# Which engine splits the weights and adds the compression offsets in a two-layer fp32 trunk: GpSimd's shares of the first mixer and of the MLP starts given to VectorE

## The chip, the cores and the metric

One NeuronCore of a Trainium2 chip runs the whole program. Its engines each work through an own queue in order: TensorE (PE; PEld is its weight load), VectorE (DVE), ScalarE (ACT), GpSimd (POOL), and SyncE (SP), which here issues the weight DMAs. Semaphores tie the queues together. The metric is the device time of one execution in microseconds, lower is better.

## The reference

The trunk has 256 tokens of width 1024 and two layers. Each layer is a token mixer and a squared-ReLU MLP, each behind an RMS norm whose scale, shift and gate come from a conditioning vector. The first mixer is a sparse attention with a compressed branch; the second is a differential attention, which the change does not touch. The parts that matter here:

```python
def compress_blocks(blk, pe, w1, w2):          # blocks of 32 tokens, one every 16
    z = (blk + pe[:, None, :]).transpose(0, 1, 3, 2, 4).reshape(B, NC, NSA_GROUPS, CMP_BLOCK * HEAD_DIM)
    return jax.nn.silu(z @ w1) @ w2
...
for i in range(DEPTH):
    mod = cond @ w_ada[i] + b_ada[i]
    ...
    x = x + g1[:, None, :] * y                  # y: the mixer's output
    h = rms_norm(x, ln_mlp_g[i]) * (1.0 + sc2[:, None, :]) + sh2[:, None, :]
    x = x + g2[:, None, :] * (jnp.square(jax.nn.relu(h @ w_mlp_in[i])) @ w_mlp_out[i])
```

Everything is fp32. `compress_blocks` is called once for keys and once for values; there are 15 blocks, 4 groups.

## The kernel before

**Split weights.** An fp32 product is made of three matmuls over halves. `mm3` (L78 to L83) issues them: L81 is high half times high half, L82 and L83 are the two cross products; the name on the right of an `out<-in` says which tiles they read. A weight tile `wr` (128x1024 fp32, 512 KB) comes by a DMA that SP issues. `do_unit` (L190 to L233) turns it into a "unit": the high half `wh` is a cast on ACT (L202), the low half `wl` is `wr` minus `wh`, one `tensor_tensor` (L206), on VectorE or on GpSimd. Which of the two is read from the list `halves[0]`: split number p takes entry p modulo the length of the list. `use(u)` (L241) hands a unit to the matmuls and first splits the units that lie up to `look[0]` ahead, so a split is emitted some units before its product. Splits carry a lowered priority; the Tile scheduler then fixes one order per engine, and that order is what the queues run.

**Where the list stands before.** `sublayer_end` sets `[(act.copy, vec)]` at the end of each sublayer: VectorE alone. Before each mixer the main program sets two entries, so every second split goes to POOL. `mlp` sets three entries with one on POOL ahead of `up_first(nb)`, which computes the first two 512-wide blocks of the hidden layer.

**The first mixer.** `proj_rows` multiplies the normed input by the weight units; `kv_post` (L900) norms and rotates keys (`head_norms` L796, L805 to L814; `rope` L775, L781 to L785; statistics `hns`, `hnm`, `hnt`, `hnr`), computes the gates (`gz`, `gates`, L894 to L898) and transposes the keys on PE (`heads_T`, L793). `compress` (L912) makes `z`, the block inputs plus offsets (L917 memset, L920 sums), multiplies them (L927) and applies the activation (`he`, L931 to L933). Attention scores follow, with `mn` (L1014), `pr` (L1043) on DVE. The vector `acc` of the conditioning projection is summed in between from its own weight tiles on DVE (L227, L232): `acc` plus `wr` times a column, tile after tile, in DVE's order.

**The MLP start.** `prenorm` (L1143) norms the residual per token half t and in quarters: L561 to L572 (statistics `lnss`, POOL's power `lnr` at L570, scaled rows at L572), PE transposes (L1151), scale and shift (L1156 on DVE, L1159 on ACT), then `hh` (high half, L1163) and `hl` (low half, L1164). `up_first` multiplies them block by block, L81 to L83 with out `sc`, transposes the activated blocks back (L1229) and splits them (L76 on ACT, L77 on DVE, out `z`).

All tiles of 128x1024 (`wh`, `wl`, `z`, `acc`) come from one ring of 32.

Of the kernel before, what the change touches and what calls it, by code (L numbers as in the profile page):

```python
# [23 lines left out]
ALU = mybir.AluOpType  # L24
# [3 lines left out]
P = 128  # L28
# [14 lines left out]
def body(ctx: ExitStack, tc: tile.TileContext, a):  # L43
    nc = tc.nc
    vec, act, pool, pe = nc.vector, nc.scalar, nc.gpsimd, nc.tensor
# [9 lines left out]
    def bank(tag="tr"):  # L55
        return pp.tile([P, 512], F32, name=tag, tag=tag, bufs={"acc": 4, "sc": 2, "tr": 2}[tag])

    def tmp():
        return tp.tile([P, 512], F32, name="t", tag="t", bufs=6)

    def w4(name, dt=F32):

        return wp.tile([P, 1024], dt, name=name, tag="w", bufs=32)
# [4 lines left out]
    def z4():  # L68
        return w4("z4", F32R).rearrange("p (i s) -> p i s", i=4)

    def small(shape, name, bufs=3, dt=F32):
        return sp.tile(shape, dt, name=name, tag=name, bufs=bufs)
# [18 lines left out]
    halves = [[(act.copy, vec)]]  # L91
# [149 lines left out]
    def use(u, only=False):  # L241

        ahead = look[0] if only else 0
        for v in range(u, len(units)):
            if units[v][0] == "w":
                ahead += 1
                if v > u and ahead > look[0] - 1:
                    break
            done_to(v)
            if only:  # L250
                break
        h, l = done.pop(u)
        return lambda c, w: (h[:, c : c + w], l[:, c : c + w])
# [48 lines left out]
    def rsqrt_mean(ss, w, shape, name, bufs=3):  # L302

        m, r, t = (small(shape, name + c, bufs) for c in "mrt")
        vec.tensor_scalar(m, ss, 1.0 / w, EPS, op0=ALU.mult, op1=ALU.add)
        act.activation(t, m, AF.Ln)
        act.activation(r, t, AF.Exp, scale=-0.5)
        vec.tensor_tensor(t, r, r, op=ALU.mult)
        vec.tensor_tensor(t, t, m, op=ALU.mult)
        vec.tensor_scalar(t, t, -0.5, 1.5, op0=ALU.mult, op1=ALU.add)  # L310
        vec.tensor_tensor(r, r, t, op=ALU.mult)
        return r
# [344 lines left out]
    def kv_products(k):  # L657
        wu = [done.pop(u) for u in U["kv", k]]

        def w_(c, n):  # L660
            return tuple(z[:, c % 1024 : c % 1024 + n] for z in wu[c // 1024])

        st, sp_ = k == 0, k == KT - 1
        x_ = hh[:, k], hl[:, k]
        for bk, c0 in ((b_kc, 0), (b_vc, 256)):
            for m in range(2):
                mm3(bk[:, m * S : (m + 1) * S], w_(c0 + m * P, P), x_, st and m == 0, sp_)
        yield
        for t in range(2):
            ts = slice(t * P, (t + 1) * P)  # L670
            x_ = hh[:, k, ts], hl[:, k, ts]
            mm3(b_ks[:, t * 256 : t * 256 + 256], x_, w_(512, 256), st and t == 0, sp_)
            mm3(b_m[t][:, 0:256], x_, w_(768, 256), st, sp_)
            mm3(b_m[t][:, 256:512], x_, w_(1024, 256), False, sp_)
            mm3(b_v[t][:, 0:304], x_, w_(1280, 304), st, sp_)
            yield

    kc2 = []
# [59 lines left out]
    for k in range(KT):  # L738
        g = kv_products(k)
# [29 lines left out]
    pe2 = (cols[:, 0:16], cols[:, 16:32])  # L769
# [142 lines left out]
    def compress():  # L912

        hb = bank()
        for kv in range(2):
            z = w4("z").rearrange("p (m g c) -> p m g c", m=16, g=4)
            pool.memset(z[:, :, :, 15], 0.0)  # L917
            for mh in range(2):
                for g in range(4):
                    pool.tensor_tensor(z[:, 8 * mh : 8 * mh + 8, g, 0:15],  # L920
                                      kc2[kv][:, g, 8 * mh : 8 * mh + 120].rearrange("p (c m) -> p m c", m=8),
                                      pe2[kv][:, 8 * mh : 8 * mh + 8][:, :, None].to_broadcast([P, 8, 15]), op=ALU.add)
            zs.append(z)
            yield 0
        for m in range(16):
            for kv in range(2):
                pe.matmul(hb[64 * kv : 64 * kv + 64, 0:P], zs[kv][:, m].rearrange("p g c -> p (g c)"),  # L927
                          w1c[2 * kv + m // 8][:, m % 8], start=m == 0, stop=m == 15, skip_group_check=True)
        he = small([P, P], "he", 1)
        act.activation(he, hb[:, 0:P], AF.Exp, scale=-1.0)  # L930
        vec.tensor_scalar(he, he, 1.0, None, op0=ALU.add)  # L931
        vec.reciprocal(he, he)
        vec.tensor_tensor(he, hb[:, 0:P], he, op=ALU.mult)  # L933
        yield 1
        tb = bank()
        pe.transpose(tb[:, 0:P], he, ident)
        hid = small([P, 4, 16], "hid", 1)
        vec.tensor_copy(hid.rearrange("p g c -> p (g c)"), tb[:, 0:64])
        hidv = tmp()[:, 0:256].rearrange("p (q i c) -> p q i c", q=2, i=4)
        vec.tensor_copy(hidv, tb[:, 64:P].rearrange("p (q c) -> p q c", q=2)[:, :, None, :].to_broadcast([P, 2, 4, 32]))  # L940
        yield 1
        kb = bank()
        for h in range(2):
            pe.matmul(kb[64 * h : 64 * h + 64, 0:32], w2c[0], hid.rearrange("p (gp h) c -> p h gp c", h=2)[:, h],
                      start=True, stop=True, skip_group_check=True)
        sq = small([P, 32], "csq", 1)
        act.activation(sq, kb[:, 0:32], AF.Square)

        for gp in range(2):
            vb = bank()  # L950
            pe.matmul(vb[:, 0:64], hidv[:, gp].rearrange("p i c -> p (i c)"), w2c[1], start=True, stop=True)
            vec.tensor_tensor(vt[gp][:, 512:1024].rearrange("p (e d) -> p e d", e=8),
                              vb[:, 0:64][:, None, :].to_broadcast([P, 8, 64]),
                              own[:, :, None].to_broadcast([P, 8, 64]), op=ALU.mult)
        yield 1
        sb = bank()
        pe.matmul(sb[:, 0:32], bdones, sq, start=True, stop=True)
        rr = rsqrt_mean(sb[:, 0:32], 64, [P, 32], "cr", 1)
        for h in range(2):
            ps_ = slice(64 * h, 64 * h + 64)  # L960
            vec.scalar_tensor_tensor(kcbd[ps_, :, h, :], kb[ps_, 0:32].rearrange("p (g c) -> p g c", g=2),
                                     gk0[ps_], rr[ps_].rearrange("p (g c) -> p g c", g=2), op0=ALU.mult, op1=ALU.mult)
        yield 0
# [232 lines left out]
    def mlp(l):  # L1196
# [4 lines left out]
        def relu2(bk):  # L1201
            r = tmp()
            act.activation(r, bk, AF.Relu)  # L1203
            s2 = tmp()
            act.activation(s2, r, AF.Square)
            return s2

        def up_first(nb):

            zs = [(z4(), z4()) for _ in range(nb)]  # L1210
            hid.update(enumerate(zs))
            ws = {}

            def products(b, t):
                ts = slice(t * P, (t + 1) * P)
                if t == 0:
                    ws[b] = [[use(u) for u in U["up", l, b, f2]] for f2 in range(2)]
                bk = bank("sc")
                for f2 in range(2):
                    for k in range(KT):  # L1220
                        mm3(bk[:, f2 * 256 : f2 * 256 + 256], (hh[:, k, ts], hl[:, k, ts]),
                            ws[b][f2][k // 4](k % 4 * 256, 256), k == 0 and f2 == 0, k == KT - 1)
                return relu2(bk)

            def back(b, t, s2):
                ts = slice(t * P, (t + 1) * P)
                tb = bank()
                for j in range(4):
                    pe.transpose(tb[:, j * P : (j + 1) * P], s2[:, j * P : (j + 1) * P], ident)  # L1229
                split(zs[b][0][:, :, ts], zs[b][1][:, :, ts], tb.rearrange("p (j s) -> p j s", j=4))  # L1230

            prev = None
            for t in range(2):
                for b in range(nb):
                    s2 = products(b, t)
                    if prev is not None:
                        back(*prev)
                    prev = (b, t, s2)
            back(*prev)
# [51 lines left out]
                    yield t, 2  # L1291

        look[0], ahead_dma[0] = 6, 14
        halves[0] = [(act.copy, pool), (act.copy, vec), (act.copy, vec)]
        nb = 2
        up_first(nb)
        while held:
            held.pop(0)()
        for b in range(1, NB):
# [4 lines left out]


    look[0], ahead_dma[0] = 4, 10
    halves[0] = [(act.copy, pool), (act.copy, vec)]
    cg = compress()
    next(cg)
    next(cg)  # L1310
# [194 lines left out]
```

## Time and profile before

| | us |
|---|---|
| median of 3 runs | 722.15 |
| lowest, highest | 720.5, 722.8 |
| the profiled execution, by its own time | 721.25 |
| its span (first to last recorded instruction) | 719.1 |
| PE busy | 682.3 (95%) |
| DVE busy | 493.1 (69%) |
| ACT busy | 400.5 (56%) |
| POOL busy | 200.5 (28%) |

The profiled execution takes 2.15 us more than its span; both parts lie inside its 721.25. Busy shares are means over the whole program; the views by stretch tell where an engine is short. The clock row of the page gives TensorE's granted clock: 1.00 is the upper of its two levels, 2.4 GHz, and 0.50 the lower, 1.2 GHz.

### The profile page before, as it was taken

What the parts mean: (1) busy time and instruction counts of PE and PEld (TensorE: products, weight loads), DVE (VectorE), ACT (ScalarE), POOL (GpSimd) and SP (SyncE); (2) the same over time, 40 slices, a digit from 0 to 9 for tenths busy, and PEclk for the clock granted to TensorE, in tenths of its full rate; (3) what the DMA queues carried; (4) which work ended last, traced back from release to release, by engine and by line L of the source; (5) the groups of instructions that cost most, each with busy time, mean ns of one, the idle gap of its engine ahead of it and who ended that gap; (6) DMA issues with size and microseconds to landing.
All of it is one profiled execution on the core that took longest, in us unless ns stands there. A gap on an engine that the chain in (4) does not pass through costs nothing.

```text
span 719.1 us, 11663 instructions
## 1 busy us (share of the span) xinstructions
PE 682.3 (95%) x4263; PEld 565.1 (79%) x4263; DVE 493.1 (69%) x911; ACT 400.5 (56%) x779; POOL 200.5 (28%) x138
## 2 busy tenths in 40 slices
PE   8999889999988999999999999899979999999997
PEld 7787654656687988999896777667769888998896
DVE  4457879777869598858885987776782874235753
ACT  6646438769565345634453765786566355543650
POOL 4105311002023243233231634223222143323430
PEclk9999999999999999999999999999999999999999
DMA  9999999522828889989799254243744787755001
GB/s 289 331 334 373 325 307 289 150 75 91 263 87 274 279 298 370 331 286 319 262 358 350 81 159 170 94 118 92 243 164 138 261 280 229 231 180 176 1 1 58
DMA packets 105421, 156.67 MB, mean 218 GB/s; under 512 B 6135, under 2 KB 60180, under 8 KB 105364
## 3 DMA queue, kind: packets, MB, share of 16 engines
q1 hardware_dynamic: 103952, 153.60, 65.9%
q0 software_dynamic: 1248, 2.20, 1.1%
q8 instruction: 33, 0.54, 0.3%
q14 instruction: 24, 0.20, 0.1%
q10 hardware_dynamic: 164, 0.14, 0.1%
HBM read 154.86 MB, written 1.06 MB: 217 GB/s over the span
## 4 chain that ended last, share of the span: by engine, by line
PE 59%; DVE 17%; issue 11%; DMA 4%; ACT 4%; POOL 2%; SPq 1%; DVEq 0%; POOLq 0%; ACTq 0%
PE acc L83 9%; PE acc L81 8%; PE acc L82 8%; PE sc L83 8%; PE sc L81 7%; PE sc L82 7%; DVE wl L206 5%; DMA wr<-in_nsa_w_in_dram 3%; DVE acc L232 2%; PE sc L1008 1%; PE tr L172 1%; ACT wh L202 1%; PE tr L1048 1%; SPq L158 1%; POOL wl L206 1%
## 5 line engine op out<-in xcount | busy, mean ns | idle before, releaser
L206 POOL TENSOR_TENSOR wl<-wr,wh 128x1024 fp32r<-128x1024 f32 x60 | 157.5, 2628 | 363.2 <-ACT wh L202 298.0
L206 DVE TENSOR_TENSOR wl<-wr,wh 128x1024 fp32r<-128x1024 f32 (+1 forms) x132 | 188.5, 1443 | 63.3 <-ACT wh L202 46.2
L202 ACT CAST wh<-wr 128x1024 fp32r<-128x1024 f32 x192 | 191.9, 1032 | 47.4 <-PE acc L82 10.0
L81 PE MATMUL acc<-wh,z 128*128 128x512 f32 (+1 forms) x320 | 127.5, 398 | 0.0
L83 PE MATMUL acc<-wh,z 128*128 128x512 f32 (+1 forms) x320 | 125.2, 392 | 1.1 <-DVE z L77 1.1
L82 PE MATMUL acc<-wl,z 128*128 128x512 f32 (+1 forms) x320 | 125.2, 391 | 0.0
L81 PE MATMUL sc<-hh,wh 128*128 128x256 f32 x384 | 109.0, 284 | 0.0
L83 PE MATMUL sc<-hh,wl 128*128 128x256 f32 x384 | 108.7, 283 | 0.0
L82 PE MATMUL sc<-hl,wh 128*128 128x256 f32 x384 | 108.7, 283 | 0.0
L1203 ACT ACTIVATE t<-sc 128x512 f32<-128x512 f32 x32 | 19.1, 598 | 109.6 <-PE sc L83 109.5
L81 PEld LDWEIGHTS sc<-hh,wh 128*128 128x128 f32 x384 | 73.6, 192 | 1.3 <-issue 0.8
L82 PEld LDWEIGHTS sc<-hl,wh 128*128 128x128 f32 x384 | 73.7, 192 | 0.4
L232 DVE SCALAR_TENSOR_TENSOR acc<-wr,cond,acc 128x1024 f32<-128x1024 f32 x49 | 72.4, 1477 | 2.2 <-DMA wr<-in_w_ada_dram 1.5
L83 PEld LDWEIGHTS sc<-hh,wl 128*128 128x128 f32 x384 | 73.6, 192 | 0.0
L83 PEld LDWEIGHTS acc<-wh,z 128*128 128x128 f32 x320 | 60.1, 188 | 14.2 <-DVE z L77 2.0
L81 PEld LDWEIGHTS acc<-wh,z 128*128 128x128 f32 x320 | 60.2, 188 | 13.7 <-issue 1.9
L82 PEld LDWEIGHTS acc<-wl,z 128*128 128x128 f32 x320 | 60.2, 188 | 11.5 <-issue 0.6
L77 DVE TENSOR_TENSOR z<-t,z 128x512 fp32r<-128x512 f32 x24 | 26.7, 1113 | 60.3 <-ACT z L76 60.3
L82 PE MATMUL acc<-wl,hh 128*128 128x512 f32 (+1 forms) x160 | 61.1, 382 | 3.0 <-DVE wl L206 3.0
L81 PE MATMUL acc<-wh,hh 128*128 128x512 f32 (+1 forms) x160 | 63.1, 396 | 0.0
L83 PE MATMUL acc<-wh,hl 128*128 128x512 f32 (+1 forms) x160 | 60.5, 378 | 0.0
L83 PE MATMUL sc<-wh,hl 128*128 128x256 f32 (+1 forms) x152 | 44.1, 292 | 4.2 <-DVE hl L1164 4.1
(286 smaller groups left out, 1119.4 us busy)
## 6 DMA issues: line engine op xcount, KB each, us to landing
wr<-in_w_ada_dram SPq DMA_DIRECT2D x80, 512.0 KB, 5.9
wr<-in_w_mlp_in_dram SPq DMA_DIRECT2D x64, 512.0 KB, 4.9
wr<-in_w_mlp_out_dram SPq DMA_DIRECT2D x64, 512.0 KB, 4.4
wr<-in_diff_w_in_dram SPq DMA_DIRECT2D x24, 512.0 KB, 5.1
wr<-in_w_ada_dram SPq DMA_DIRECT2D x32, 256.0 KB, 6.8
wr<-in_nsa_w_in_dram SPq DMA_DIRECT2D x16, 512.0 KB, 7.3
wr<-in_nsa_w_out_dram SPq DMA_DIRECT2D x16, 256.0 KB, 10.4
wr<-in_diff_w_out_dram SPq DMA_DIRECT2D x8, 512.0 KB, 3.7
```

The lines of the kernel that those rows point to most:

```text
L77: vec.tensor_tensor(l, src, h.bitcast(F32), op=ALU.subtract)
L81: pe.matmul(out, x[0], w[0], start=start, stop=False, skip_group_check=True)
L82: pe.matmul(out, x[0], w[1], start=False, stop=False, skip_group_check=True)
L83: pe.matmul(out, x[1], w[0], start=False, stop=stop, skip_group_check=True)
L158: nc.sync.dma_start(f(raws[i]), src)
L172: pe.matmul(ps[32 * c : 32 * c + 32, 0:n], condz[:, k], w, start=k < 4, stop=k >= 4, skip_group_check=True, tile_position=(0, 32 * c))
L202: hi(h, r[:, 0:n])
L206: lo.tensor_tensor(l, r[:, 0:n], h.bitcast(F32), op=ALU.subtract)
L232: vec.scalar_tensor_tensor(st["acc"], r, c, st["acc"], op0=ALU.mult, op1=ALU.add)
L1008: pe.matmul(p1, q[:, P:S], k, start=True, stop=True)
L1048: pe.transpose(tb[:, e * P : (e + 1) * P], s.pr[:, br, h, e * P : (e + 1) * P], ident)
L1203: act.activation(r, bk, AF.Relu)
```

## The change

Three edits. The sums of the compression are four VectorE instructions of 480 columns instead of sixteen GpSimd instructions of 120 (the memsets of `z` stay on POOL). The list with one POOL entry in three is set behind `up_first` instead of ahead of it, so all splits that `up_first` emits, the units ahead that it looks at too, are VectorE's. The two-entry list ahead of the first mixer is gone; there the list of one entry holds. The second mixer keeps its own.

```diff
             for mh in range(2):
-                for g in range(4):
-                    pool.tensor_tensor(z[:, 8 * mh : 8 * mh + 8, g, 0:15],
-                                      kc2[kv][:, g, 8 * mh : 8 * mh + 120].rearrange("p (c m) -> p m c", m=8),
-                                      pe2[kv][:, 8 * mh : 8 * mh + 8][:, :, None].to_broadcast([P, 8, 15]), op=ALU.add)
+                vec.tensor_tensor(z[:, 8 * mh : 8 * mh + 8, :, 0:15],
+                                  kc2[kv][:, :, 8 * mh : 8 * mh + 120].rearrange("p g (c m) -> p m g c", m=8),
+                                  pe2[kv][:, 8 * mh : 8 * mh + 8][:, :, None, None].to_broadcast([P, 8, 4, 15]), op=ALU.add)
...
         look[0], ahead_dma[0] = 6, 14
-        halves[0] = [(act.copy, pool), (act.copy, vec), (act.copy, vec)]
         nb = 2
         up_first(nb)
+        halves[0] = [(act.copy, pool), (act.copy, vec), (act.copy, vec)]
...
     look[0], ahead_dma[0] = 4, 10
-    halves[0] = [(act.copy, pool), (act.copy, vec)]
     cg = compress()
```

On POOL ten of the 60 splits leave: six in the first mixer and two at each MLP start. Numbers behind names tell apart tiles of one name; the numbering differs between the kernels.

**DVE, keys of the first mixer.** `wl_998` before and `wl_986` after are the low half of the third weight unit of this stretch, `wl_1018` (POOL before) and `wl_1006` that of the fourth. Before:

```order
L897 RECIPROCAL gates_942<-gz_1039 128x48
L898 TENSOR_SCALAR gcmp_943<-gates_942,consts_76 128x16 x2
L308 TENSOR_TENSOR hnt_989<-hnr_988 128x16
L206 TENSOR_TENSOR wl_998<-wr_575,wh_997 128x1024
L309 TENSOR_TENSOR hnt_989<-hnt_989,hnm_987 128x16
L310 TENSOR_SCALAR hnt_989<-hnt_989 128x16
L311 TENSOR_TENSOR hnr_988<-hnr_988,hnt_989 128x16
```

After:

```order
L206 TENSOR_TENSOR wl_917<-wr_569,wh_916 128x1024
L728 TENSOR_TENSOR csg_296<-trig_213,gbg_276 128x64
L919 TENSOR_TENSOR z_951<-t_897,cols_685 128x32x15 x2
L919 TENSOR_TENSOR z_955<-t_902,cols_685 128x32x15 x2
L805 TENSOR_REDUCE hns_961<-t_966 128x4
L805 TENSOR_REDUCE hns_961<-t_969 128x4
L805 TENSOR_REDUCE hns_961<-t_972 128x4
L894 TENSOR_TENSOR gz_1021<-sc_292,gbg_276 128x48
L305 TENSOR_SCALAR hnm_975<-hns_961 128x16
L894 TENSOR_TENSOR gz_1027<-tr_293,gbg_276 128x48
L206 TENSOR_TENSOR wl_986<-wr_575,wh_985 128x1024
L308 TENSOR_TENSOR hnt_977<-hnr_976 128x16
```

The four sums stand ahead of the third unit's split, and the gate work (`gates`, `gcmp`) has moved behind it.

**PE, the same place.** `acc` with `wl_1018` (before) and `wl_1006` (after) are products of the fourth unit, `tr<-first,qn` the transposes of the keys. Before:

```order
L81 MATMUL acc_972<-wh_1017,hh_138 128x512
L793 MATMUL tr_1069<-first_75,qn_974 128x128 x4
L793 MATMUL tr_1078<-first_75,qn_974 128x128 x4
L82 MATMUL acc_972<-wl_1018,hh_138 128x512
L83 MATMUL acc_972<-wh_1017,hl_139 128x512
```

After:

```order
L81 MATMUL acc_959<-wh_1005,hh_138 128x512
L81 MATMUL acc_960<-wh_1005,hh_138 128x512
L81 MATMUL acc_1165<-wh_1041,hh_138 128x512
L82 MATMUL acc_959<-wl_1006,hh_138 128x512
L83 MATMUL acc_959<-wh_1005,hl_139 128x512
L793 MATMUL tr_1057<-first_75,qn_962 128x128 x4
L793 MATMUL tr_1066<-first_75,qn_962 128x128 x4
```

The transposes have moved ahead by five matmuls of 512 columns, to near the start of the fourth unit.

**DVE, start of the first MLP.** The second `hh` and `hl` of the first token half, `t_2350` before and `t_2338` after; `wl_2412` after is the third unit, which was POOL's. Before:

```order
L206 TENSOR_TENSOR wl_2412<-wr_2015,wh_2411 128x1024
L572 TENSOR_SCALAR t_2365<-xt_82,lnr_2363 128x512
L206 TENSOR_TENSOR wl_2418<-wr_2107,wh_2417 128x1024
L1163 CAST hh_138<-t_2350 128x4x128
L1156 TENSOR_SCALAR t_2374<-tr_2369,mA01_131,mB01_132 128x128
L1164 TENSOR_TENSOR hl_139<-t_2350,hh_138 128x4x128
```

After:

```order
L206 TENSOR_TENSOR wl_2400<-wr_2003,wh_2399 128x1024
L563 SCALAR_TENSOR_TENSOR lnss_2296<-lnss_2296 128x1
L206 TENSOR_TENSOR wl_2406<-wr_2095,wh_2405 128x1024
L1162 CAST hh_138<-t_2338 128x4x128
L572 TENSOR_SCALAR t_2353<-xt_82,lnr_2351 128x512
L1163 TENSOR_TENSOR hl_139<-t_2338,hh_138 128x4x128
L206 TENSOR_TENSOR wl_2412<-wr_2148,wh_2411 128x1024
```

The split that was POOL's stands on DVE behind `hl`, not ahead of it. At the second MLP it does too, and PE's order there is as it was.

## Rows read from the trace of the kernel before

**Rows 1.** Windows: stretch, its length, busy of each engine, PEclk, DMA share, GB/s
```profile
70.00:90.00 20.00, 16.35 (x115) 12.87 (x113) 17.20 (x29) 8.94 (x16) 8.95 (x10) 0.91 1.08 323
110.00:130.00 20.00, 18.52 (x104) 10.51 (x104) 17.92 (x92) 17.55 (x67) 2.41 (x1) 1.00 1.06 292
235.00:390.00 155.00, 154.45 (x982) 136.72 (x981) 115.83 (x97) 72.13 (x93) 48.49 (x22) 1.00 0.91 318
```
**Rows 2.** Waits of PE, 55 to 105: us in total, times, longest
```profile
PE acc L82 <- DVE wl L206: 2.4, 2, 1.8
```
**Rows 3.** Waits of PE, 105 to 200
```profile
PE sc L1008 <- DVE mn L1014: 1.1, 2, 0.6
```
**Rows 4.** Waits of PE, 200 to 300
```profile
PE sc L83 <- DVE hl L1164: 1.8, 1, 1.8
PE tr L1229 <- DVE z L77: 1.6, 1, 1.6
PE acc L83 <- DVE z L77: 0.8, 1, 0.8
```
**Rows 5.** Waits of PE, 490 to 560
```profile
PE sc L83 <- DVE hl L1164: 2.3, 2, 1.8
```
**Rows 6.** POOL in order of time: start, us, instruction, idle before and releaser
```profile
64.38 5.41 POOL L920 TENSOR_TENSOR z<-t,cols 128x120 f32<-128x120 f32 x8
74.17 2.37 POOL L206 TENSOR_TENSOR wl<-wr,wh 128x1024 fp32r<-128x1024 f32 x1
...
202.11 2.38 POOL L206 TENSOR_TENSOR wl<-wr,wh 128x1024 fp32r<-128x1024 f32 x1 [1.83 <-ACT wh L202]
```
**Rows 7.** DVE in order of time, first mixer
```profile
67.68 0.48 DVE L728 TENSOR_TENSOR csg<-trig,gbg 128x64 f32<-128x64 f32 x1
...
71.93 1.53 DVE L206 TENSOR_TENSOR wl<-wr,wh 128x1024 fp32r<-128x1024 f32 x1
...
74.28 2.31 DVE L311 TENSOR_TENSOR hnr<-hnr,hnt 128x16 f32<-128x16 f32 x1
...
77.95 1.69 DVE L781 TENSOR_TENSOR ropeA<-qn,csg 128x128 f32<-128x128 f32 x2
79.56 0.48 DVE L781 TENSOR_TENSOR ropeB<-qn,csg 128x128 f32<-128x128 f32 x2
79.97 1.21 DVE L206 TENSOR_TENSOR wl<-wr,wh 128x1024 fp32r<-128x1024 f32 x1
...
95.72 0.17 DVE L311 TENSOR_TENSOR hnr<-hnr,hnt 128x16 f32<-128x16 f32 x1
...
97.24 1.97 DVE L310 TENSOR_SCALAR crt<-crt 128x32 f32<-128x32 f32 x1
...
176.39 3.16 DVE L1043 TENSOR_SCALAR pr<-pr,sm 128x128 f32<-128x128 f32 x4
...
179.80 0.99 DVE L1043 TENSOR_SCALAR pr<-pr,sm 128x128 f32<-128x128 f32 x4
```
**Rows 8.** PE in order of time, at the key transposes
```profile
79.35 0.39 PE L83 MATMUL acc<-wh,hl 128*128 128x512 f32 x1
79.58 0.39 PE L81 MATMUL acc<-wh,hh 128*128 128x512 f32 x1
81.64 1.09 PE L793 MATMUL tr<-first,qn 128*128 128x128 f32 x8 [1.67 <-DVE qn L785]
```
**Rows 9.** DVE in order of time, start of the first MLP
```profile
197.65 0.69 DVE L1164 TENSOR_TENSOR hl<-t,hh 128x512 fp32r<-128x512 f32 x1
...
202.51 2.53 DVE L1164 TENSOR_TENSOR hl<-t,hh 128x512 fp32r<-128x512 f32 x1
...
216.86 2.52 DVE L227 TENSOR_SCALAR acc<-wr,cond 128x1024 f32<-128x1024 f32 x1 [6.61 <-PE sc L83]
```
**Rows 10.** Windows (columns as in Rows 1), the spells below full clock
```profile
76.00:78.00 2.00, 2.00 (x6) 1.52 (x6) 1.97 (x6) 1.04 (x1) 1.66 (x2) 0.50 1.04 377
...
536.00:538.00 2.00, 2.00 (x12) 2.00 (x11) 1.87 (x4) 1.43 (x2) 0.00 (x0) 0.50 0.00 0
```

## The prediction

> **What bounds the kernel now.** I read the windows by stretch first. From 235 to 390, in the body of the first MLP, PE is busy for 154.45 of 155 us at granted clock 1.00 [rows 1]. There POOL and DVE can be as late as they like; what the change moves there is worth nothing. The stretches where PE is short are the mixers and the MLP starts: 16.35 of 20 us between 70 and 90, with DVE at 17.20 and POOL at 8.95, and 18.52 of 20 between 110 and 130, with DVE at 17.92 [rows 1]. Next the waits of PE in those stretches: it waits 2.4 us for low halves of weights between 55 and 105 [rows 2], and 1.67 us for the rotated keys `qn` ahead of their transposes at 81.64 [rows 8]; 1.8 us for `hl`, 1.6 and 0.8 us for `z` at the first MLP's start [rows 4]; 2.3 us for `hl`, one wait 1.8 of it, around the second MLP's start [rows 5]. Every one of these releasers is DVE. Each wait removed with nothing late behind it is time gained.
>
> Then DVE's rows at those waits, to see why DVE is late. The 16-column `hnr` (L311) takes 2.31 us at 74.28, and 0.17 us at 95.72 [rows 7]. POOL splits a weight from 74.17 for 2.37 us, to 76.54 [rows 6]: `hnr` ends at 76.59, just behind it. `hl` takes 0.69 us at 197.65 and 2.53 us at 202.51, ending at 205.04 [rows 9]; POOL splits from 202.11 to 204.49 [rows 6]. So a DVE instruction that starts while POOL works in SBUF stands still until POOL is done. Other rows look the same: `pr` 3.16 us against 0.99 [rows 7], `ropeA` 1.69 against 0.48 for `ropeB` of the same size [rows 7], `crt` at 1.97 [rows 7], L227 at 2.52 [rows 9]. In the trace a POOL split of about 2.4 us costs DVE up to its own length, while the same split as DVE's own work is 1.21 us [rows 7]. This is the argument for a gain: in a stretch where DVE is the releaser, taking a split over can be cheaper for DVE than standing beside POOL's.
>
> Last the windows on the clock. PE runs at 0.50 (1.2 GHz) from 76 to 78 and from 536 to 538 [rows 10]; 2 us at half rate lose 1.0 us of full-rate work. Each follows a wait of PE of 1.8 us, for a low half [rows 2] and for `hl` [rows 5]; the wait of 1.8 us for `hl` at the first MLP [rows 4] and that of 1.67 us for the keys [rows 8] have none behind them. Two of four: I count a spell as even after such a wait.
>
> **The change, part by part. First, the keys of the first mixer (64 to 82).** The sums cost DVE 4 instructions of 480 columns. The nearest row is `hl`, two SBUF inputs and 512 columns, 0.69 us [rows 9]: 480/512 of it is 0.65, so 2.6 us in all. The upper bound comes from POOL: 8 sums take 5.41 us [rows 6], so four, the work of one new instruction, take 2.7; a POOL split takes 2.37 against DVE's 1.21, a ratio of 2, so 1.35 each and 5.4 in all. I take 2.6, because the same-engine row is nearer.
>
> One rule of the Trainium skill speaks against that. The sums read their input with a step of 8 fp32 values, 32 bytes, whereas `hl` reads in a row. The page "SBUF — State Buffer", section "Door 1: The DMA port swizzle", notes 16-byte lines, and that each access that crosses to a new line pays a penalty; here every element would. No row of this trace shows a DVE read with that step; if the penalty doubled the read, an estimate from that page's note would be 1.3 us each, the mixer's term below would become a loss, and the sum would be some 3 us smaller.
>
> Now the chain. Between the end of `csg` (68.16) and the start of the fourth split in DVE's order (79.97) there are 11.8 us, of which the third split is 1.53 [rows 7], so 10.3 us of other work. Of these go the hold on `hnr`, 2.31 − 0.17 = 2.1, and that on `ropeA`, 1.69 − 0.48 = 1.2 [rows 7]. The statistics and gate instructions between 68 and 74 run beside POOL's sums and are slower too; I estimate 1.5 us back on them, with 0 as the bound. That leaves 5.5 us. By the new order the sums go ahead of the third split; from 68.16 it is 2.6 (sums) + 1.2 (third split) + 5.5 = 77.5 for the start of the fourth, 78.7 for its end. Two short instructions follow, so the key transposes start at 79.3 instead of 81.64 [rows 8]. PE's order has put five 512-column matmuls behind them that were in front; two of them in a row start 0.23 us apart [rows 8], so 1.15 us are still to do. Gain 81.64 − 79.3 − 1.15 = 1.2 us. With sums at 5.4 and no 1.5 back, it is 1.2 − 2.8 − 1.5 = −3.1; with the `hnr`-like relief reaching all of it, about +1.7. The wait on the third unit shrinks only a little, and a new wait of some 2 us arises at the fourth unit's low half; it is inside this number. The split that was POOL's at 76.89 now follows the transposes on DVE; PE then has the fourth unit's remaining products to work on, so I count it at nothing, and at 1.2 us if that cover is gone.
>
> **Second, the rest of the mixer (82 to 190).** Four POOL splits become DVE's, 4 × 1.21 = 4.8 us. The one at 97 held `crt` (1.97 us, such small ones take 0.17, so 1.8 back) and the one at 177 held `pr` (3.16 − 0.99 = 2.2 back) [rows 7]: these two gain DVE 1.6 together. The one near 110 falls into DVE at 17.92 of 20 busy [rows 1], where PE waits 1.1 us for `mn` [rows 3]: up to 1.2 lost. The one near 166 I count at nothing, and at 1.2 if PE turns out to wait for it: among the waits of that stretch, of which the longest on DVE are such as `mn`, none is for a split. I take 0 in all, between +1.6 gained and 2.4 lost.
>
> **Third, the first MLP's start.** The hold on `hl` goes: POOL's split of 202.11 is DVE's behind `hl`. The second `hl` would end about 202.6, and the two splits ahead of it in DVE's order stood ahead of it before too. The 1.8 us wait goes [rows 4]. The half-done products of the second token half gain nothing from it: their `hh` comes behind two splits now, but PE has whole blocks of the first half to do. Further on, L227 stood 2.52 us beside POOL's second split [rows 9], and the two `z` waits of 1.6 and 0.8 [rows 4] come behind that on DVE. The split takes 1.21 on DVE instead; about half of 2.4 should go, 1.2, with bounds 0 and 2.4. Together 3.0.
>
> **Fourth, the second MLP's start.** PE's order is the same, and DVE's split has moved behind `hl`: the 1.8 us go [rows 5]. The spell at 0.50 behind it (1.0 us [rows 10]) goes with an even chance, 0.5. Together 2.3. What hides the splits added here is PE's queue of first-half products.
>
> **The sum.** 1.2 + 0 + 3.0 + 2.3 = 6.5 us, off the profiled execution's own 721.25 (span 719.1 and 2.15 around it): 714.7. The median before, 722.15, is 0.9 higher, within the spread of its three runs; I don't shift for that. Nothing after the starts takes it back: the body of the MLP is PE's alone [rows 1].
>
> **Rivals.** *The clock and new waits.* PE meets two waits in the keys' stretch, of about 1 and 2 us, and a spell at 0.50 follows: 1.0 lost. The spell at the second MLP stays, 0.5 less, and the `z` waits stay, 1.2 less. 6.5 − 2.7 = 3.8, so 717.4. For it: two such spells are in the trace [rows 10]. Against: the waits before them are what the change shortens.
>
> *Everything goes.* Mixer 1.7 + 1.6, first MLP 1.8 + 2.4, second 1.8 + 1.0: 10.3, so 710.9. For it: every one of these waits has DVE as its releaser. Against: the mixer's DVE is at 86 to 90% [rows 1], and adds work.
>
> *The sums are dear.* At 1.35 us each the third and fourth splits come late, the keys' stretch loses 3.1, and the rest of the mixer 0.5 more; the MLP starts give only the two `hl` waits, 3.6. Time 721.2: no change.
>
> *DVE becomes the mixer's bound (the slower side).* Six splits, 7.3 us, and sums of 5.4 add 12.7 us to DVE between 64 and 190. If the holds that end give back only `hnr` and `pr` (2.1 + 2.2), as other waits stand ready behind `ropeA` and `crt`, the mixer pays 8.4; less 3.6 from the MLPs, 726.0. It decides from a net mixer cost of 3.6 + 2.2 = 5.8 us on. For it: DVE is 90% busy from 110 to 130 [rows 1]. Against: from 150 on DVE has room, so the splits there hide, and POOL's holds are seen on the very rows.
>
> **How the numbers follow.** Forecast (712 to 716) 0.45; the clock and new waits 0.22; everything goes 0.13; sums dear 0.12; DVE bound 0.08. A measurement of this kernel can tell 0.3%, 2.2 us, from no change. So faster 0.80, same 0.12, slower 0.08. The time is that of the forecast, 714.7. The range from 710.5 to 719.8 leaves out the DVE bound (0.08), most of the dear sums and the low end of everything.
>
> **What would show it.** Right: `hl` near 0.7 us at both MLP starts and no PE wait there; `hnr` near 0.2; the sums at 0.6 to 0.7 us each; key transposes near 79. Wrong: sums above 1 us; a new PE wait of over 2 us on `wl` near 76 with a spell at 0.50 behind it; PE waiting longer for `mn` around 110 to 130, or for `z` at the first MLP.

## The result

| | before | after |
|---|---|---|
| median of 13 runs, us | 722.42 | 716.33 |
| lowest to highest, us | 719.19 to 724.56 | 713.05 to 719.47 |
| the profiled execution, us (span) | 721.25 (719.1) | 713.05 (711.3) |

The ratio is 0.9925, with a 95% interval of 0.9903 to 0.9947: 5.4 us faster, between 3.8 and 7.0. The forecast was 714.7, that is 6.5 us off the profiled execution. The profiled execution of after happens to be its fastest run, so the two traces differ by 8.2 us, more than the kernels do. Places are read from the traces below, the worth of an edit from the timed runs.

The page of after, part 1. To be read against it: DVE had 493.1 us for 911 instructions before.

```profile
PE 678.2 (95%) x4263; PEld 562.3 (79%) x4263; DVE 492.3 (69%) x925; ACT 399.6 (56%) x779; POOL 166.9 (23%) x112
```

DVE took over ten splits (12 us by their own length) and the sums (4 us), and its busy time did not rise. So before, about that much of DVE's busy time was standing still beside POOL.

DVE of after, in order of time, at the places of [rows 7] and [rows 9] (start, us, instruction, idle before and releaser):

```profile
67.96 4.01 DVE L919 TENSOR_TENSOR z<-t,cols 128x480 f32<-128x480 f32 x4
...
75.19 0.12 DVE L311 TENSOR_TENSOR hnr<-hnr,hnt 128x16 f32<-128x16 f32 x1
...
200.73 0.69 DVE L1163 TENSOR_TENSOR hl<-t,hh 128x512 fp32r<-128x512 f32 x1
...
214.50 0.75 DVE L227 TENSOR_SCALAR acc<-wr,cond 128x1024 f32<-128x1024 f32 x1
...
526.98 0.69 DVE L1163 TENSOR_TENSOR hl<-t,hh 128x512 fp32r<-128x512 f32 x1
```

`hnr` takes 0.12 us where it took 2.31, `hl` 0.69 at both MLP starts where it took 2.53, L227 0.75 where it took 2.52. A sum takes 1.00 us. PE's waits of after, 200 to 300, the answer to [rows 4]:

```profile
PE acc L83 <- DVE z L77: 1.0, 1, 1.0
```

The wait for `hl` at the first MLP is gone, and of the 2.4 us for `z` 1.4. For 490 to 560, the answer to [rows 5], one row is of interest: the long wait there is gone, the short one is left.

```profile
PE sc L83 <- DVE hl L1163: 0.5, 1, 0.5
```

And PE's waits from 55 to 105 and 105 to 200, the answers to [rows 2] and [rows 3]:

```profile
PE acc L82 <- DVE wl L206: 4.2, 3, 2.3
...
PE sc L81 <- DVE hh L1162: 2.3, 1, 2.3
PE sc L1007 <- DVE mn L1013: 1.5, 2, 1.0
```

In the first mixer PE waits longer for low halves (4.2 us against 2.4), and at the mixer's end it waits 2.3 us for `hh`. Of before's lists, three rows belong beside these:

```profile
PE tr L793 <- DVE qn L785: 1.7, 1, 1.7
PE tr L793 <- DVE kcbd L961: 1.3, 1, 1.3
...
PE sc L81 <- DVE hh L1163: 1.4, 1, 1.4
```

The waits for the keys `qn` and for `kcbd` (a tile of compressed keys) are gone, so up to 105 the three kinds together, 5.4 us, became 4.2. The wait for `hh` was 1.4. PE of after at the key transposes, the answer to [rows 8]:

```profile
74.24 0.50 PE L82 MATMUL acc<-wl,hh 128*128 128x512 f32 x1 [2.32 <-DVE wl L206]
...
78.90 0.50 PE L82 MATMUL acc<-wl,hh 128*128 128x512 f32 x1 [1.42 <-DVE wl L206]
...
79.47 1.04 PE L793 MATMUL tr<-first,qn 128*128 128x128 f32 x8
```

The wait on the third unit has grown from 1.8 to 2.32 us, the one on the fourth is new, and the transposes start at 79.47.

Behind the wait for `hh` the granted clock falls in after, as the windows show (stretch, its length, busy of each engine, PEclk, DMA share, GB/s):

```profile
196.00:198.00 2.00, 1.78 (x8) 1.66 (x9) 1.97 (x4) 2.00 (x4) 0.00 (x0) 0.60 0.58 199
198.00:200.00 2.00, 2.00 (x12) 2.00 (x12) 1.89 (x4) 2.00 (x5) 1.51 (x1) 0.54 0.00 0
```

So the two spells of [rows 10] are gone in this execution and a new one, some 1.7 us of work (2 x 0.40 + 2 x 0.46), has come. Of the second spell in before, [rows 10] shows one window; its neighbours are

```profile
534.00:536.00 2.00, 1.97 (x14) 1.98 (x15) 1.74 (x4) 1.61 (x4) 0.00 (x0) 0.87 0.04 8
...
538.00:540.00 2.00, 2.00 (x15) 2.00 (x15) 1.19 (x1) 0.12 (x1) 0.00 (x0) 0.78 0.00 0
```

so that one too took 1.7 us of work (2 x 0.13 + 2 x 0.50 + 2 x 0.22).

### The profile page after: what moved, and what is told of

It is laid out like the page before. It is cut to its first block, busy times and chain, and to the rows that moved or that the text cites. A ratio compares the mean times of both kernels' runs of the same rounds, so it can differ in the third digit from the quotient of the medians.

```text
span 711.3 us, 11653 instructions
## 1 busy us (share of the span) xinstructions
PE 678.2 (95%) x4263; PEld 562.3 (79%) x4263; DVE 492.3 (69%) x925; ACT 399.6 (56%) x779; POOL 166.9 (23%) x112
## 4 chain that ended last, share of the span: by engine, by line
PE 60%; DVE 15%; issue 9%; DMA 7%; ACT 4%; POOL 2%; SPq 2%; DVEq 0%; POOLq 0%; ACTq 0%
PE acc L83 8%; PE acc L82 8%; PE acc L81 8%; PE sc L81 8%; PE sc L83 8%; PE sc L82 8%; DVE wl L206 5%; DMA wr<-in_nsa_w_out_dram 3%; DMA wr<-in_w_ada_dram 3%; SPq L158 2%; PE sc L1007 1%; PE tr L1047 1%; ACT wh L202 1%; DVE acc L232 1%; POOL wl L206 1%
## 5 line engine op out<-in xcount | busy, mean ns | idle before, releaser
L206 DVE TENSOR_TENSOR wl<-wr,wh 128x1024 fp32r<-128x1024 f32 (+1 forms) x142 | 198.1, 1410 | 66.8 <-ACT wh L202 59.2
L206 POOL TENSOR_TENSOR wl<-wr,wh 128x1024 fp32r<-128x1024 f32 x50 | 133.2, 2666 | 275.1 <-ACT wh L202 210.9
L232 DVE SCALAR_TENSOR_TENSOR acc<-wr,cond,acc 128x1024 f32<-128x1024 f32 x49 | 74.9, 1528 | 4.0 <-DMA wr<-in_w_ada_dram 3.4
L81 PE MATMUL sc<-wh,hh 128*128 128x256 f32 (+1 forms) x152 | 44.5, 294 | 2.9 <-DVE hh L1162 2.9
```

Source lines behind the costliest of these rows:

```text
L81: pe.matmul(out, x[0], w[0], start=start, stop=False, skip_group_check=True)
L206: lo.tensor_tensor(l, r[:, 0:n], h.bitcast(F32), op=ALU.subtract)
L232: vec.scalar_tensor_tensor(st["acc"], r, c, st["acc"], op0=ALU.mult, op1=ALU.add)
```

## The experiments

The theory (H): a split on POOL holds DVE's instructions in SBUF until it is done, and that costs time where PE waits for DVE. Rivals: the gain is the first mixer's (M); it comes from the new order of instructions or from earlier low halves, not from the hold (O). All ratios are to the kernel before, taken on the same chip in turns, with their 95% intervals.

### The three edits one at a time

**The sums alone.** The kernel before, with

```diff
-                for g in range(4):
-                    pool.tensor_tensor(z[:, 8 * mh : 8 * mh + 8, g, 0:15],
...
+                vec.tensor_tensor(z[:, 8 * mh : 8 * mh + 8, :, 0:15],
```

> The kernel before with one edit: the compression sums are the four VectorE instructions; all splits stay where they were. Theory H (the holds of DVE by POOL's splits are what costs): the splits still hold hnr, crt, pr and hl, so hl stays at 2.5 us at both MLP starts; the four sums add 4.0 us to DVE but the statistics between 68 and 74 run free of POOL's sums. Time the same within 1 us, ratio 0.999 to 1.002. Rival M (the mixer's part of the gain comes from taking the sums off POOL): key transposes at about 79.5 as in the changed kernel, time 2 us lower, ratio 0.997.

1.0006 (0.9988 to 1.0024): no difference. DVE at the keys shows the holds moved rather than removed:

```profile
75.60 2.12 DVE L310 TENSOR_SCALAR hnt<-hnt 128x16 f32<-128x16 f32 x1
77.64 0.44 DVE L897 RECIPROCAL gates<-gz 128x48 f32<-128x48 f32 x1
78.00 2.08 DVE L311 TENSOR_TENSOR hnr<-hnr,hnt 128x16 f32<-128x16 f32 x1
```

POOL, with no sums, does its two splits from 75.29 to 80.05 one behind the other, and two 16-column instructions of DVE stand beside them for 2.1 us each. What rival M credits to the sums falls.

**The first mixer's splits alone.**

```diff
     look[0], ahead_dma[0] = 4, 10
-    halves[0] = [(act.copy, pool), (act.copy, vec)]
```

> The kernel before with one edit: the first mixer's splits are all VectorE's; the sums stay on POOL and the MLPs keep their list. Theory H: hnr, crt and pr near 0.2, 0.2 and 1.0 us; the keys' transposes about 2 us earlier than before, the rest of the mixer gives 0 to 1 us back; the first MLP start keeps its hl hold. Time 1 to 2 us lower, ratio 0.997 to 0.9985. Rival M: with the sums still on POOL nothing is gained in the keys' stretch, ratio 1.000 or above.

0.9997 (0.998 to 1.0015): no difference (by the interval a gain of 1.4 us at most), where theory H as I wrote it expected 1 to 2 us. With this, what rival M credits to the mixer's splits falls too. The keys' stretch does get shorter (the table below), so something gives it back.

**The MLP edit alone.**

```diff
-        halves[0] = [(act.copy, pool), (act.copy, vec), (act.copy, vec)]
         nb = 2
         up_first(nb)
+        halves[0] = [(act.copy, pool), (act.copy, vec), (act.copy, vec)]
```

> The kernel before with one edit: the list with a POOL entry is set behind the first two blocks of each MLP. Theory H: hl at 0.7 us at both MLP starts, PE's 1.8 us waits gone at both, some of the z waits gone at the first MLP, the half-rate spell at the second MLP gone: 3 us at the first and 2 to 3 at the second, time 5 to 6 us lower, ratio 0.992 to 0.993. Rival M: only the two waits go, 3.6 us, ratio 0.995, the rest of the change's gain being the mixer's.

0.9916 (0.99 to 0.9932), 715.29 us. That is 6.1 us, within the intervals all of the change's gain.

**The sums back on POOL** in the changed kernel:

> The changed kernel with one edit undone: the compression sums are the sixteen POOL instructions again. Theory H: the sums on DVE cost 4.0 us of DVE ahead of the third split and free about as much for the small instructions beside them, so this kernel is within 1 us of the changed one, ratio to the kernel before 0.992 to 0.994. Rival M: without the sums' edit the keys' stretch loses its 2 us, ratio 0.995 to 0.996.

0.9927 (0.9908 to 0.9945). Whether sixteen POOL instructions or four of DVE make the sums cannot be told in the time.

### Is it the hold?

The MLP edit changes the order of the instructions too, so the next two kernels keep the changed order and add work to POOL that nobody reads, when the splits go by that used to be POOL's (two at each MLP start):

```diff
             with tc.high_priority(-50):
                 hi(h, r[:, 0:n])
+            if extra[0] and pos["split"] % 3 == 0:
+                with tc.high_priority(-50):
+                    spare = w4("spare")
+                    pool.tensor_tensor(spare[:, 0:n], r[:, 0:n], h.bitcast(F32), op=ALU.subtract)
```

> The changed kernel with POOL's two splits of each MLP start added again as extra work that nobody reads (VectorE's splits stay, the extra tiles come from the ring of 32). Theory H (POOL's split holds DVE's two-input instructions): hl is 2 to 2.5 us at the second MLP's start and held at the first one too, PE waits for hl 1.8 us at the second and up to 1.8 at the first, and the time is 2 to 5 us above the changed kernel: ratio 0.995 to 0.999. Rival O (the gain is the new order of the instructions on DVE and PE, or the earlier low halves): nobody waits for the extra work, hl stays 0.7, ratio 0.991 to 0.994.

0.9996 (0.9973 to 1.0019), 721.62 us: the whole gain is lost. At the second MLP POOL and DVE in order of time:

```profile
531.73 2.38 POOL L207 TENSOR_TENSOR spare<-wr,wh 128x1024 f32<-128x1024 f32 x1 [1.83 <-ACT wh L203]
```
```profile
532.12 2.54 DVE L1168 TENSOR_TENSOR hl<-t,hh 128x512 fp32r<-128x512 f32 x1
```

`hl` stands until POOL is done, as in [rows 9]. PE's waits at the first MLP's start, 198 to 240:

```profile
PE tr L1155 <- DVE t L577: 1.8, 1, 1.8
PE tr L1233 <- DVE z L77: 1.5, 1, 1.5
PE acc L83 <- DVE z L77: 1.2, 1, 1.2
```

There it is not `hl` that is caught but the scaled row `t` (L577, 2.59 us), and both `z` waits are back. Rival O falls: the order was kept (DVE's 925 instructions come, by name, as in after; on PE two pairs near 225 change places), and the gain is gone.

The second kernel has POOL write only, two memsets behind a one-column difference:

```diff
+                    pool.tensor_tensor(spare[:, 0:1], r[:, 0:1], h.bitcast(F32)[:, 0:1], op=ALU.subtract)
+                    pool.memset(spare, 0.0)
+                    pool.memset(spare, 0.0)
```

> As the kernel before it in this list, but POOL's extra work is a one-column difference and two memsets of the same tile, which write SBUF and read nothing. The Trainium skill, page SBUF — State Buffer, section Who interferes with whom, says that a DVE instruction with two SBUF inputs meets only a GpSimd operation that reads SBUF. By that hl stays 0.7 us and the ratio is the changed kernel's, 0.991 to 0.994. If any POOL work in SBUF holds DVE, hl is 1.5 to 2.5 us and the ratio 0.995 to 0.999.

0.9912 (0.988 to 0.9945). POOL and DVE at the second MLP:

```profile
530.06 0.96 POOL L208 MEMSET spare<- 128x1024 f32 x1
531.08 0.96 POOL L209 MEMSET spare<- 128x1024 f32 x1
```
```profile
530.19 0.69 DVE L1170 TENSOR_TENSOR hl<-t,hh 128x512 fp32r<-128x512 f32 x1
```

`hl` runs inside the first memset and takes its 0.69 us. So POOL's being busy does not hold `hl`; POOL's reading of SBUF tiles does. The Trainium skill, page "SBUF — State Buffer", section "Who interferes with whom", says just that: VectorE and GpSimd share a pair of ports by an exclusive lock, held for a whole instruction by whichever came first, and a VectorE instruction with two SBUF inputs contends only with a GpSimd instruction that reads SBUF. The traces agree on both sides, 2.54 us against 0.69.

That the read decides is shown for `hl`, which has two inputs. Instructions with one input are held by a split too (`t` above, 2.59 us against 0.49 in after), and one of them took longer beside a memset:

```profile
217.73 1.07 DVE L234 TENSOR_SCALAR acc<-wr,cond 128x1024 f32<-128x1024 f32 x1
```

It takes 0.75 in after. For these the runs do not tell a read from a write.

### Why the first mixer's edits buy nothing

From the trace of each kernel I took four starts on PE: the last product of two high halves with 304 columns (the end of the keys' and gates' weights), the first of the compression, the first score product and the first product of the MLP. In after these are 64.66, 82.13, 107.17 and 196.22. The stretches between them, in us:

| kernel | first mixer | keys | to the scores | to the MLP | sum |
|---|---|---|---|---|---|
| before | as before | 19.95 | 25.22 | 88.15 | 133.3 |
| sums alone | sums on DVE | 22.42 | 24.72 | 88.14 | 135.3 |
| MLP edit alone | as before | 20.66 | 25.43 | 88.18 | 134.3 |
| mixer's splits alone | splits on DVE | 16.75 | 28.37 | 89.71 | 134.8 |
| sums back on POOL | splits on DVE | 16.61 | 26.48 | 89.24 | 132.3 |
| after | both edits | 17.47 | 25.04 | 89.05 | 131.6 |
| POOL memsets | both edits | 17.45 | 26.37 | 90.06 | 133.9 |

The keys' stretch is 2.5 to 4 us shorter with the splits on DVE than in before and with the MLP edit alone; the sums on DVE take back 0.8 of it. But not all of that is gain: by the new order five matmuls of 512 columns, 1.15 us at 0.23 each [rows 8], stand behind the stretch's end instead of in it (47 against 52 there, 49 against 44 in the next). Like for like the keys gain 1.3 to 2.9 us, and the stretch to the scores, with those 1.15 us taken off, is anything from 1.5 us shorter to 2.0 longer. The one to the MLP is 0.9 to 2 longer. DVE's waits from 75 to 140 name a cause. With the mixer's splits alone:

```profile
DVE acc L232 <- DMA wr<-in_w_ada_dram: 3.3, 2, 2.3
```

and in after:

```profile
DVE acc L232 <- DMA wr<-in_w_ada_dram: 0.9, 2, 0.6
```

The sums of the conditioning vector stand in DVE's order between the mixer's own instructions. Pulled forward, DVE reaches them before their weight tiles have landed; the DMA engines are at their limit there (share 1.04 to 1.08), so the tiles don't come earlier, and `he` and later `mn` queue behind. Before, no such row stands in that list, and with the MLP edit alone one of 0.7 us. The eight traces with the mixer's splits on DVE and full tiles all have it, with 0.9 to 3.3 us, and nothing else on PE, DVE or ACT waits for a DMA between 64 and 200 in them; how long the wait is differs by execution. The first sum that waits, in after:

```profile
84.10 1.28 DVE L232 SCALAR_TENSOR_TENSOR acc<-wr,cond,acc 128x1024 f32<-128x1024 f32 x1 [0.59 <-DMA wr<-in_w_ada_dram]
```

and the same one before, which waits for nothing:

```profile
84.62 1.28 DVE L232 SCALAR_TENSOR_TENSOR acc<-wr,cond,acc 128x1024 f32<-128x1024 f32 x1
```

To tell this from the other candidates (the split near 110, the longer wait for `hh`), the next pair of kernels loads those tiles an eighth. Seven eighths of that part of the conditioning projection are left out.

```diff
-            items.append([(whole, a["w_ada"][l, k * P : (k + 1) * P, c0 : c0 + 1024])])
+            if light[0] is st:
+                items.append([(lambda r: r[:, 0:P], a["w_ada"][l, k * P : (k + 1) * P, c0 : c0 + P])])
+            else:
+                items.append([(whole, a["w_ada"][l, k * P : (k + 1) * P, c0 : c0 + 1024])])
```

On the changed kernel:

> The changed kernel with the eight weight tiles of the conditioning projection that VectorE sums during the first mixer loaded an eighth: 128 of 1024 columns, repeated in the sums, so seven eighths of that row are left out; the order of instructions is the changed kernel's. 3.7 MB less are to be moved between 60 and 120. Theory D (what the first mixer's edits gain at the keys is given back because DVE's sums then stand waiting for tiles that are still on their way, and the scores' minima behind them): DVE waits for no tile there any more, and this kernel is 2 to 3 us faster than the next one, which has the first mixer of before. Rival L (it is given back by the splits on DVE near 110 and by the longer wait for hh at the mixer's end): the two differ by 1 us or less.

And on the kernel with the MLP edit alone:

> The kernel before with the MLP edit alone, and with the same eight tiles loaded an eighth: the first mixer of before with the lighter load. It is the partner of the run before: the difference between the two is what the first mixer's edits are worth without late tiles. Theory D: this one 2 to 3 us slower (0.003 to 0.004 in the ratio). Rival L: within 1 us. Against the MLP edit alone (0.9916) it also shows what the late tiles cost the old order: little, since no DVE sum waited there.

712.74 us, 0.9872 (0.9847 to 0.9896), and 715.07 us, 0.9908 (0.9884 to 0.9932). With the light tiles the first mixer's edits are worth 2.3 us by the medians, and the runs don't overlap (711.98 to 713.48 and 713.97 to 717.96); with the full ones they are worth nothing (716.33 with them, 715.29 without). DVE waits for no tile in the first of the two. The lighter load itself gives the changed kernel 3.6 us and its partner 0.2, and the changed kernel's runs lie within 1.5 us instead of 6.4 (5 runs and 13). That is what theory D expected. It makes room for all other transfers as well, so the pair alone does not prove that it is these sums; that they are the only ones in the traces to wait for a tile speaks for it. It is not quite all: the stretch to the MLP stays 0.6 us longer with the edits (88.77 against 88.13), and the wait for `hh` stays 2.3.

A second price is the clock. In seven of the nine traces with the first mixer's splits on DVE, a spell near 0.5 follows the 2.3 us wait for `hh`; of the five with the mixer as before, where that wait is 1.4 us, one has a spell that begins 2 us behind it, the kernel with the MLP edit and the light tiles. The mean granted clock of the runs says the same: 0.998 to 1.0 in the six runs of the MLP edit alone, 0.993 to 0.998 in the 13 of the whole change. A spell as in after takes 1.7 us of full-rate work, but the time loses less. With both the mixer's splits on DVE and the MLP edit, and without extra POOL splits, five traces with such a spell take 26.55 to 27.10 us from the first product of the MLP to the first of its down projection (after 26.85), the two without one 26.13 and 26.14: 0.4 to 1.0 us. In the keys' stretch it costs nothing: with a spell in it 17.45 (POOL memsets), 17.45 and 17.51 us (two kernels below), without one 17.47 in after. There PE's wait of 1.42 us at 78.90 is missing in the three, so the slower matmuls fill time that PE would have waited.

### The order of the sums' elements

```diff
-                vec.tensor_tensor(z[:, 8 * mh : 8 * mh + 8, :, 0:15],
-                                  kc2[kv][:, :, 8 * mh : 8 * mh + 120].rearrange("p g (c m) -> p m g c", m=8),
...
+                vec.tensor_tensor(z[:, 8 * mh : 8 * mh + 8, :, 0:15].rearrange("p m g c -> p g c m"),
+                                  kc2[kv][:, :, 8 * mh : 8 * mh + 120].rearrange("p g (c m) -> p g c m", m=8),
```

> The changed kernel with one edit: the four sums run through the same 480 elements in another order, so that the input is read in a row and the output is written with the step. If the step on the read is what makes a sum 1.00 us instead of 0.65, the sums come to 0.65 us each, 1.4 us less of DVE ahead of the third split; if it is the step as such, or the length of the inner row, they stay near 1.0 or rise. In the whole time, theory D (the keys' stretch is held by weight tiles that land late, so DVE's time there buys nothing): the ratio stays as that of the changed kernel, 0.991 to 0.994. Rival: 1.4 us less, 0.990.

0.9909 (0.9875 to 0.9943), which holds both expectations of the time, and the four sums:

```profile
68.59 3.65 DVE L919 TENSOR_TENSOR z<-t,cols 128x480 f32<-128x480 f32 x4
```

0.91 us instead of 1.00. The step on the read alone isn't what lifts a sum from 0.65 to 1.00; with it moved to the write, most of the price stays. Whether it is the step as such or the short inner rows is open.

### The same hold elsewhere

If POOL's splits hold DVE where PE waits for DVE, the second mixer should gain as the MLP starts did:

```diff
     look[0], ahead_dma[0] = 6, 8
-    halves[0] = [(act.copy, pool), (act.copy, vec)]
```

> The changed kernel with the second mixer's POOL splits given to VectorE too. Theory H: ropeB (2.6 us in the second mixer beside POOL's splits, three times) falls to about 0.5, PE's waits for qn (2.9 us) and dmn (1.7) shrink, and the eleven splits of 1.2 us cost DVE 13 us where it is busy 8 of 10: a gain of 1 to 3 us on the changed kernel, ratio 0.988 to 0.991. Rival B (DVE becomes the bound of the second mixer): new waits of PE on wl, ratio 0.995 or more.

0.9822 (0.9787 to 0.9857), 709.05 us: 7.3 us below the changed kernel and 12.5 below the one before, more than twice what I expected at most. DVE in the second mixer, with the MLP edit alone and then with this one:

```profile
417.67 1.56 DVE L781 TENSOR_TENSOR ropeA<-qn,csg 128x256 f32<-128x256 f32 x1
419.15 2.61 DVE L781 TENSOR_TENSOR ropeB<-qn,csg 128x256 f32<-128x256 f32 x1
```
```profile
413.07 0.42 DVE L781 TENSOR_TENSOR ropeA<-qn,csg 128x256 f32<-128x256 f32 x1
413.40 0.42 DVE L781 TENSOR_TENSOR ropeB<-qn,csg 128x256 f32<-128x256 f32 x1
```

PE's waits from 385 on, through the second mixer, in the same two kernels:

```profile
PE tr L793 <- DVE qn L785: 2.9, 4, 1.5
PE sc L1007 <- DVE dmn L1014: 1.7, 1, 1.7
PE tr L1375 <- DVE z L1402: 1.5, 1, 1.5
PE tr L1375 <- DVE pr L1369: 1.5, 1, 1.5
```
```profile
PE tr L793 <- DVE qn L785: 1.3, 1, 1.3
PE tr L1372 <- ACT pr L1356: 0.7, 1, 0.7
```

The four longest, 7.6 us, become 2.0, of which 0.7 are new and on ACT. The new bound that rival B expected does not appear: PE's wait for `wl` there is 0.6 us in both, and DVE's busy time over the whole kernel falls from 492.3 to 484.9 us with 14 splits more (I had counted eleven).

Dropping the list in the MLP bodies too, so that POOL splits nothing:

> The kernel of the run before this (second mixer on VectorE too) with the list of the MLP bodies dropped as well: no split is POOL's any more. Theory H in its full form (a POOL split costs only where PE waits for what DVE does beside it): in the MLP bodies PE waits for nothing, so nothing is to be gained, and DVE, busy 109 of 150 us there, takes 22 splits of 1.2 us more and still ends in time: the time of the run before within 2 us, ratio 0.980 to 0.985. Rival F (holds cost everywhere): a further 2 to 5 us, ratio 0.975 to 0.979. Rival G (DVE becomes the bound of the bodies): new waits of PE on wl there, ratio 0.987 or more.

0.9845 (0.982 to 0.9871), 710.73 us: as the kernel with POOL's splits there, within the intervals. The window from 235 to 385, first with POOL's splits in the bodies, then without:

```profile
235.00:385.00 150.00, 149.45 (x959) 132.56 (x959) 109.22 (x95) 70.16 (x91) 47.41 (x21) 1.00 0.91 318
```
```profile
235.00:385.00 150.00, 150.00 (x960) 133.29 (x959) 107.05 (x111) 70.93 (x90) 2.10 (x4) 1.00 0.92 317
```

POOL's share goes from 47 us to 2, DVE does 16 instructions more, and DVE's busy time falls by 2 us. Even where nobody waits, POOL's splits take nothing off DVE.

Last, the two edits that work, without the first mixer's:

> The kernel before with the MLP edit and with the second mixer's splits on VectorE; the first mixer as before (its POOL splits and POOL sums). If the first mixer's two edits are worth nothing in the whole time, as the single edits read (1.0006 and 0.9997), the ratio is that of the kernel with both, 0.980 to 0.984. If they are worth the 1 to 2 us that the stages of the profiled executions show, the ratio is 0.983 to 0.986.

0.9841 (0.9816 to 0.9867), 710.61 us. It can't be told from the kernel with all of them; the interval holds both expectations.

## Why the prediction was right, and where it was not

The sum was 6.5 us and the kernels differ by 5.4 (3.8 to 7.0), but not term by term. That it comes so near is in part luck: the MLP starts gave 0.8 us more than forecast, and the first mixer, forecast at 1.2, gave nothing that the time shows.

- **Both MLP starts** were forecast at 3.0 + 2.3 = 5.3; the edit alone measures 6.1. From the first product of the MLP to the first of its down projection, the stretch shrinks from 30.2 to 26.56 at the first MLP (the MLP edit alone), 3.6 us: 1.8 for `hl`, 1.6 for the first `z` wait, and 0.3 that no row explains. The second `z` wait, behind that stretch, grew from 0.8 to 1.0, so of the two 1.4 went where I took 1.2. At the second it shrinks from 30.37 to 27.04, 3.3, in which the spell at 0.50 is whole; in the two traces without that spell and without the edit it was 28.9, so the wait alone is 1.9. Counting the spell at an even chance was fair (two of the four traces with that wait have one), but its size was not: 1.0 us is what one window of [rows 10] loses; with its neighbours it is 1.7 us of work, of which 1.5 show in that stretch (30.37 against 28.9). The mechanism, a POOL split holding DVE, is shown by the two kernels with POOL work that nobody reads. "While POOL works in SBUF" was too wide: a memset does not hold `hl`.
- **The keys of the first mixer** were forecast at 1.2. The step in which I sized the sums at 0.65 by the nearest row failed: they are 1.00, and 1.4 us more of DVE lay ahead of the third split. PE's wait for that split did not shrink a little but grew, from 1.8 to 2.32 us. The other step erred the other way: I left 5.5 us for the small instructions, and from the sums' end at 71.97 to the fourth split at 77.62 they take 4.4 beside the third split's 1.2. So the fourth split starts at 77.62, where 77.5 was forecast, by two errors that cancel: luck. The stretch became 2.5 us shorter, or 1.3 with the five matmuls that I had counted as still to do.
- **The rest of the first mixer** was forecast at 0 and gives back what the keys won: in the whole time the edits are worth nothing. I had priced the split near 110 and the held `pr` and `crt`, but not that DVE's sums of the conditioning vector, in order with the rest, would find their tiles still on the way, nor that PE, arriving earlier, would wait longer for `hh` and lose its clock behind it. The trace of before had it to read: the sum that waits until 84.10 in after ran at 84.62 before, so the path could come forward by about half a microsecond there before it met the tile.
- **The rivals.** Of "the clock and new waits" the two waits at the keys came (2.32 and 1.42 us). The spell came in after at another place than I gave, ahead of the MLP; in the three traces that have it at the keys it costs nothing. "The sums are dear" was right on the sums, at 1.00 us, and wrong on the consequence: with the sums back on POOL the time is the same (0.9927 against 0.9925). "DVE becomes the mixer's bound" is not what happened: in that stretch the splits on DVE shorten the keys' path in every trace. "Everything goes" was right on the second MLP.
- **The signs that I had named.** Of those for right came `hl` near 0.7, `hnr` near 0.2 and the transposes near 79; the sums at 0.6 to 0.7 did not. Of those for wrong came a wait of over 2 us on `wl` near 76, without a spell behind it in after, and a longer one for `mn` (1.5 us against 1.1).
- **The rule on 16-byte lines** of the Trainium skill (page "SBUF — State Buffer", section "Door 1: The DMA port swizzle"), which I weighed against the sums, gives the right sign: 1.00 us instead of 0.65, between the row I used and the 1.3 by doubling. No run separates it from other reasons for the price.

## What to carry to other kernels

Before an engine is relieved by giving work to GpSimd, compare the busy time of VectorE instructions beside that work with the same instructions elsewhere: if they end just behind GpSimd's, the work was not taken off, only turned into standing still, and it hurts exactly where the critical engine waits for VectorE. Where a path is shortened, look at what else stands in the same in-order queue and waits for a DMA; if the DMA engines are full, the shorter path ends at the next tile. And time the parts of a change apart: here one edit of three carried the gain, and the same idea at a place that the change had left out was worth more than all of it.

## What the runs showed that I had not expected

- Work on POOL that nobody reads costs as much as work that is needed: four extra splits, 722 us instead of 716.
- Fourteen splits less on POOL lower DVE's busy time by 7 us, although DVE does them itself.
- A POOL write that nobody reads costs `hl` nothing (0.69 us inside a memset).
- At one place, a wait of PE of 2.3 us is followed by a spell near 0.5 in seven of nine traces, one of 1.4 us in one of five.
- A spell costs what PE could have done with it: 1.5 us at the second MLP, 0.4 to 1.0 at the first, nothing at the keys, where PE would have waited anyway.
